# Layer 0's V pass over 208 dense tokens with a second drawn group, and the early group's dots and half of its rows in the U passes

## The chip, the cores and the metric

One NeuronCore of a Trainium2 chip runs the whole program. The metric is the device time of one execution in microseconds (us). Three runs of the kernel before were timed, and one more execution was taken with the hardware profiler; every row quoted below is from that one. Engines are named as in the profile: PE is the matrix engine (PEld its weight load), DVE the vector engine, ACT the scalar engine, POOL the GpSimd engine, SP the engine that issues most of the DMA transfers.

## The reference

A two-layer encoder for 256 tokens, to which 16 learned meta tokens are prepended (272 tokens, width 1024). Layer 0 mixes tokens with a gated recurrence, layer 1 with a Conformer convolution module; each is followed by PEER, a retrieval among 16,384 experts per layer, and every sublayer ends in a LayerNorm. PEER is where nearly all the time goes:

```python
s1, i1 = lax.top_k(scores[:, :, 0], PEER_TOPK)
s2, i2 = lax.top_k(scores[:, :, 1], PEER_TOPK)
cand = (s1[..., :, None] + s2[..., None, :]).reshape(c, PEER_HEADS, PEER_TOPK * PEER_TOPK)
s, flat = lax.top_k(cand, PEER_TOPK)
expert = idx1 * PEER_N_KEYS + idx2
g = jax.nn.softmax(s.astype(jnp.float32), axis=-1).astype(xc.dtype)
act = jax.nn.gelu(jnp.einsum('chkd,cd->chk', expert_u[expert], xc))
return jnp.einsum('chk,chkd->cd', g * act, expert_v[expert])
```

So each token picks 16 experts in each of 8 heads, takes a dot product with each picked row of U, and adds up the picked rows of V with these weights. All tables are float32.

## The kernel before

**Dense passes.** For most tokens PEER is computed densely: the product with all 16,384 rows of U, a mask of gate weights g, and the product with all rows of V. U and V of a layer are each streamed from HBM as 128 tiles (index j) of 128x1024 float32, 512 KB. A tile comes into `raw` (four buffers, issued by SP in program order), ACT rounds it to `hi` (L145), DVE or POOL forms the rest `lo` = raw - hi (L152), and PE multiplies with both parts. One j of the U pass is 24 matmuls of `nu` columns (L180). One j of the V pass is 8 matmuls `hi` x [w_hi, w_lo] of 2n columns (L749) and 8 matmuls `lo` x w_hi of n columns (L753). `nu` and n are the tokens taken densely: `DENSE_U` = 240 in both layers, `DENSE_V` = 224 in layer 0 and 192 in layer 1.

**The stages.** In each layer U is passed in two halves, called U1 (j below `JA` = 64, function `u_store`) and U2 (j from 64, `u_out`), then comes V. During U2 the gates g are built in chunks of 8 tokens (`g_unit`, `one_hot`): per chunk DVE compares, multiplies and weighs (L672, L679, L680, L659), and PE does 16 matmuls (L689, L690). `chunks` covers n tokens: 28 chunks in layer 0, 24 in layer 1.

**Tokens outside the dense passes** go in groups of `FEW` = 16 tokens; 16 tokens by 8 heads fill the 128 partitions, so one rank k of the 16 is one gather of 128 rows of 4 KB (512 KB), issued by POOL (`few_rows`, L1039). There are three kinds. An *early* and a *late* group gather their U rows and take the dots on DVE (`few_mult`, L1046); a *drawn* group lies inside the 240 dense U tokens, so its activations are dumped to a table in HBM (`few_dump`, L730 and L731) and drawn from it, rank by rank (`few_draw`, L1055 and L1056). All of them gather 16 V rows and add them up on DVE (`few_add`: L1078 the first, L1080 the others); 16 matmuls per group (L788) put the sum into the accumulators of the V pass.

- Layer 0 before: early 256, late 240, drawn 224.
- Layer 1 before: early 240, no late one, drawn 224, 208 and 192.

**Where the group work stands.** The early group takes 10 dots in U1, from j = 48, and 6 in U2. All other gathers are put into V by `few_plan`: a list of rows, spread evenly over the j from 4 to 111 with two slots of run-up. The list has 64 rows in both layers. Row buffers (`rows`) are three deep in V and U1 and single in U2. DVE runs its instructions in order, so a dot or add whose row has not landed holds back the `lo` behind it. `LO_FROM` = 41 is the j of U1 from which DVE makes `lo` in place of POOL.

**Scores of the groups.** A group with tokens below 256 gets its expert numbers (`pos`) and softmax weights (`z`) through HBM: `few_spread` writes them, `few_fetch` reads them back with one row per partition. For `z` both are issued by POOL, at the end of U1.

**SBUF for the groups.** `few_load` brings the group's inputs `wide` for the dots. The early group's are loaded twice, once for U1 and again at the beginning of U2 into a pool that opens there.

The tables that steer this, and the slots of V:

```python
DENSE_U, DENSE_V = (240, 240), (224, 192)
EARLY, LATE, DRAWN = ((256,), (240,)), ((240,), ()), ((224,), (224, 208, 192))
DOTS_FROM, DOTS, AHEAD, LO_FROM = 48, 10, 2, 41
slots = len(rows) + ahead
at = [begin + s * (NK - 4 * JG - begin) // slots for s in range(slots)]
```

## Time and profile before

| | us |
|---|---|
| three timed runs | 1786.73, 1794.49, 1797.14 |
| median | 1794.49 |
| the profiled execution, device time | 1794.43 |
| its span, first to last instruction | 1792.6 |
| layer 0: U1, U2, V begin at about | 174, 350, 552 |
| layer 1: U1, U2, V begin at about | 1078, 1255, 1459 |
| mean granted PE clock | 0.994 |

| engine | busy us | share |
|---|---|---|
| PE | 1737.4 | 97% |
| DVE | 1479.4 | 83% |
| ACT | 902.9 | 50% |
| POOL | 595.6 | 33% |

The device time stands 1.8 us above the span. Matmuls are pipelined, so a busy PE need not be a PE at its best pace: the pace is read from the distance between starts. The window rows give the busy time of each engine with the number of its instructions in brackets, then the granted clock, the mean busy share of the 16 DMA engines and the bytes they moved.

### The profile page before, as it was taken

What the parts mean: (1) busy time and instruction counts of PE and PEld (TensorE: products, weight loads), DVE (VectorE), ACT (ScalarE), POOL (GpSimd) and SP (SyncE); (2) the same over time, 40 slices, a digit from 0 to 9 for tenths busy, and PEclk for the clock granted to TensorE, in tenths of its full rate; (3) what the DMA queues carried; (4) which work ended last, traced back from release to release, by engine and by line L of the source; (5) the groups of instructions that cost most, each with busy time, mean ns of one, the idle gap of its engine ahead of it and who ended that gap; (6) DMA issues with size and microseconds to landing.
All of it is one profiled execution on the core that took longest, in us unless ns stands there. A gap on an engine that the chain in (4) does not pass through costs nothing.

```text
span 1792.6 us, 35062 instructions
## 1 busy us (share of the span) xinstructions
PE 1737.4 (97%) x13452; PEld 1675.9 (93%) x13452; DVE 1479.4 (83%) x2780; ACT 902.9 (50%) x1491; POOL 595.6 (33%) x408
## 2 busy tenths in 40 slices
PE   8999999999999999999998999999899999999996
PEld 6899999999999999999887899999899999999996
DVE  7786985899997888787799869947899878888876
ACT  5554454454444545885531645444445454544452
POOL 1101993310002445431000018952211026667420
PEclk9999999999999999999999999999999999999998
DMA  5446667865557999998541356567666569999984
GB/s 200 165 140 170 187 202 235 289 218 190 171 174 266 332 327 327 322 327 283 188 141 59 106 186 180 190 236 262 223 211 196 176 219 339 343 341 347 338 314 149
DMA packets 121112, 415.41 MB, mean 232 GB/s; under 512 B 17712, under 2 KB 19056, under 8 KB 120816
## 3 DMA queue, kind: packets, MB, share of 16 engines
q1 hardware_dynamic: 94128, 324.94, 54.4%
q0 software_dynamic: 26816, 88.23, 13.2%
q8 instruction: 106, 1.74, 0.4%
q14 instruction: 62, 0.51, 0.1%
HBM read 403.98 MB, written 9.13 MB: 230 GB/s over the span
## 4 chain that ended last, share of the span: by engine, by line
PE 77%; DVE 11%; DMA 5%; ACT 3%; issue 2%; POOL 1%; DVEq 0%; POOLq 0%; SPq 0%; ACTq 0%
PE u L180 42%; PE acc L749 16%; PE acc L753 10%; DMA raw<-peer_v 4%; PE u L216 3%; DVE lo L152 2%; DVE cy L1250 2%; DVE odd L1250 2%; PE g L689 1%; PE g L690 1%; ACT hi L145 1%; POOL lo L152 1%; PE sps L578 1%; PE acc L788 1%; DVE x L363 1%
## 5 line engine op out<-in xcount | busy, mean ns | idle before, releaser
L145 ACT ACTIVATE hi<-raw 128x1024 fp32r<-128x1024 f32 x556 | 588.3, 1059 | 617.2 <-PE u L180 212.8
L152 DVE TENSOR_TENSOR lo<-raw,hi 128x1024 fp32r<-128x1024 f32 x474 | 577.1, 1222 | 161.5 <-PE u L180 88.9
L180 PE MATMUL u<-xs,hi 128*128 128x240 f32 (+2 forms) x4544 | 570.5, 277 | 0.6 <-DVE xs L379 0.6
L180 PEld LDWEIGHTS u<-xs,hi 128*128 128x128 f32 x4544 | 539.3, 190 | 1.5 <-DVE xs L379 1.0
L749 PE MATMUL acc<-w,hi 128*128 128x448 f32 (+1 forms) x1984 | 422.8, 355 | 2.4 <-DVE w L264 1.8
L749 PEld LDWEIGHTS acc<-w,hi 128*128 128x128 f32 x1984 | 347.7, 189 | 14.3 <-DVE w L264 2.2
L180 PE MATMUL u<-xs,lo 128*128 128x240 f32 (+2 forms) x2272 | 309.5, 277 | 9.9 <-DVE lo L152 6.9
L180 PEld LDWEIGHTS u<-xs,lo 128*128 128x128 f32 x2272 | 282.0, 190 | 11.8 <-DVE lo L152 7.4
L753 PEld LDWEIGHTS acc<-w,lo 128*128 128x128 f32 x2048 | 265.7, 191 | 18.3 <-DVE lo L152 13.9
L753 PE MATMUL acc<-w,lo 128*128 128x224 f32 (+1 forms) x2048 | 270.4, 273 | 9.6 <-DVE lo L152 8.4
L152 POOL TENSOR_TENSOR lo<-raw,hi 128x1024 fp32r<-128x1024 f32 x82 | 210.4, 2580 | 105.4 <-ACT hi L145 76.0
L1039 POOL DMA_INDIRECT rows<-peer_v,ids x112 | 178.5, 1594 | 189.7 <-DVE few_out L1080 115.8
L1039 POOL DMA_INDIRECT rows<-u_rows,ids x48 | 67.3, 1402 | 218.6 <-DVE rows L1046 165.6
L1080 DVE SCALAR_TENSOR_TENSOR few_out<-rows,act,few_out 128x1024 f32<-128x1024 f32 x105 | 134.6, 1281 | 3.7 <-DMA rows<-peer_v,ids 3.7
L216 PE MATMUL u<-x,raw 128*128 128x272 f32 x480 | 115.1, 399 | 5.8 <-DMA x<-h 5.8
L216 PEld LDWEIGHTS u<-x,raw 128*128 128x128 f32 x480 | 92.8, 194 | 25.9 <-DMA raw<-w_in 5.2
L730 POOL COPY own<-act_b 128x512 f32<-128x512 f32 (+2 forms) x12 | 10.3, 863 | 247.7 <-ACT act_b L705 230.9
L1056 POOL DMA_INDIRECT act<-own,turn x64 | 74.0, 1157 | 26.0 <-issue 16.5
L696 ACT ACTIVATE act_b<-g 128x488 f32<-128x488 f32 (+35 forms) x52 | 20.2, 389 | 104.1 <-DVE act_b L659 90.6
L371 POOL TENSOR_SCALAR xs<-x,par 128x272 fp32r<-128x272 f32 (+1 forms) x4 | 3.5, 882 | 185.1 <-DVE x L363 185.1
L672 DVE TENSOR_TENSOR AB<-iota,iT 128x2048 f16<-128x2048 f16 x52 | 63.5, 1225 | 0.1
L1046 DVE SCALAR_TENSOR_TENSOR rows<-rows,wide 128x1024 f32<-128x1024 f32 x48 | 58.4, 1217 | 5.2 <-DMA rows<-u_rows,ids 5.2
(283 smaller groups left out, 1794.5 us busy)
## 6 DMA issues: line engine op xcount, KB each, us to landing
raw<-peer_u SPq DMA_DIRECT2D x256, 512.0 KB
raw<-peer_v SPq DMA_DIRECT2D x248, 512.0 KB
raw<-w_query SPq DMA_DIRECT2D x28, 512.0 KB
raw<-pw SPq DMA_DIRECT2D x22, 512.0 KB
raw<-w_in SPq DMA_DIRECT2D x16, 512.0 KB
raw<-w_out SPq DMA_DIRECT2D x8, 512.0 KB
raw<-peer_v SPq DMA_DIRECT2D x16, 256.0 KB
own<-own POOLq DMA_DIRECT2D x12, 256.0 KB
```

What stands on the lines that cost most here:

```text
L145: self.act_hi = nc.scalar.activation(hi, raw, AF.Copy).ins
L152: i = e.tensor_tensor(lo[:, s], raw[:, s], hi[:, s].bitcast(F32), op=OP.subtract)
L180: self.mm = nc.tensor.matmul(ps[:, :n], l[:, k, :], xs(k, r)[:, :n], start=start, stop=stop)
L216: self.mm = self.nc.tensor.matmul(ps[:, :n], raw[:, k, :], x[:, k, :n], start=k == 0, stop=k == NB - 1)
L672: nc.vector.tensor_tensor(AB.rearrange("p x c (a b) -> p (x c) a b", b=2), keys, iT[:, c0 // HC].rearrange("p x c b -> p (x c) b")[:, :, N ...
L749: self.mm = nc.tensor.matmul(acc[b][:, :2 * n].rearrange("p (a t) -> p a t", a=2), hi, w[:, :, :n], start=j == 0, stop=j == NK - JG - 1, s ...
L753: self.mm = nc.tensor.matmul(main[b][:, :n], hi if p_ else lo, w[:, i, :n], start=False, stop=j == NK - 1 and not p_, skip_group_check=True)
L1039: self.nc.gpsimd.indirect_dma_start(out=t, out_offset=None, in_=table, in_offset=bass.IndirectOffsetOnAxis(ap=few["ids"][:, i, k:k + 1], a ...
L1046: self.nc.vector.scalar_tensor_tensor(t, t, 1.0, few["x"], op0=OP.mult, op1=OP.mult, accum_out=few["act"][:, k:k + 1])
L1056: self.nc.gpsimd.indirect_dma_start(out=few["act"][:, k:k + 1], out_offset=None, in_=few["table"].rearrange("p j (t o) -> (p j t) o", o=1) ...
L1080: nc.vector.scalar_tensor_tensor(few["out"], t, w, few["out"], op0=OP.mult, op1=OP.add)
L1250: nc.vector.scalar_tensor_tensor(z, h, w, z, op0=OP.mult, op1=OP.add)
```

## The change

Layer 0's dense V shrinks from 224 to 208 tokens, and the 16 tokens from 208 become a second drawn group there. In both layers the early group takes its dots from j = 41, 14 of them in U1 and 2 in U2, and 8 of its 16 V rows are gathered and added in U2 (`ROWS`), so that its weights (`few_weigh`) are needed there. The rows in V become 72 in layer 0 (64 + 16 - 8) and 56 in layer 1 (64 - 8). DVE takes over `lo` from j = 34. The `z` scores go over SP in place of POOL, the spread after the last load of U1 and the fetch after the load of j = 70. `wide` of the early group is loaded once, into a pool (`kp`) that lives through the layer, and that buffer becomes the place of its sum; the other groups' sums alternate between `kp` and the pool of V (`home`), which now holds one `wide` and not two. All row gathers are held in one order on POOL (`last_rows`).

```diff
-DENSE_U, DENSE_V = (240, 240), (224, 192)
-EARLY, LATE, DRAWN = ((256,), (240,)), ((240,), ()), ((224,), (224, 208, 192))
-DOTS_FROM, DOTS, AHEAD, LO_FROM = 48, 10, 2, 41
+DENSE_U, DENSE_V = (240, 240), (208, 192)
+EARLY, LATE, DRAWN = ((256,), (240,)), ((240,), ()), ((224, 208), (224, 208, 192))
+DOTS_FROM, DOTS, ROWS, AHEAD, LO_FROM = 41, 14, 8, 2, 34
...
                     if j == LO_FROM:
-                        for few in early:
-                            self.few_load(sp, few, "kept", 1)
+                        with tc.issue_after(self.last_load):
+                            self.few_load(kp, early[0], "kept")
...
-                    if j == JA - 6 - len(picked):
-                        with tc.issue_after(last.ins):
-                            self.few_spread(nc.gpsimd, near, "z", picked[0][3][:, None])
+                    if j == JA - 1:
+                        with tc.issue_after(self.last_load):
+                            self.few_spread(nc.sync, near, "z", picked[0][3][:, None])
...
-                    if j == JA - 2:
-                        with tc.issue_after(last.ins):
-                            self.few_fetch(nc.gpsimd, near, "z")
...
-                self.few_load(rp, early[0], "kept", 1)
...
+                    done = 2 + 4 * (TOPK - DOTS)
+                    if i == 6:
+                        with tc.issue_after(self.last_load):
+                            self.few_fetch(nc.sync, near, "z")
+                    if i == done:
+                        nc.scalar.activation(early[0]["act"], early[0]["act"], AF.Gelu_apprx_tanh)
+                    if i == done + 2:
+                        with tc.issue_after(self.dve_lo.ins):
+                            self.few_weigh(early[0], scale)
+                    k, step = divmod(i - done - 4, 4)
+                    if step == 0 and 0 <= k < ROWS:
+                        early[0]["rows"][k] = self.few_rows(rp, early[0], 1, k, 1)
+                    if step == 2 and 0 <= k < ROWS:
+                        with tc.issue_after(self.dve_lo.ins):
+                            self.few_add(early[0], k, kp, "kept")
...
-    def few_plan(self, vp, early, late, drawn, scale, layer, ahead=2):
+    def few_plan(self, kp, vp, early, late, drawn, scale, ahead=2):
         rows = [(few, i, k) for few in early + late + drawn for i in range(2)
-                for k in range(0 if i or few in late else TOPK, TOPK)]
+                for k in range((ROWS if few in early else 0) if i else 0 if few in late else TOPK, TOPK)]
+        for i, few in enumerate(late + drawn):
+            few["home"] = (vp, "wide") if (i + len(late)) % 2 == 0 else (kp, "kept")
+        for few in early:
+            few["home"] = kp, "kept"
```

**Layer 1, POOL, from the end of its `lo` in U1.** The rows are POOL's instructions in order; `rows<-u_rows` are the early group's dots, `z` the scores, `own` the dumps of a drawn group. Before:

```order
L152 TENSOR_TENSOR lo<-raw,hi 128x1024 x41
L1039 DMA rows<-u_rows,ids_12497 128x1024 x8
L1018 DMA z_240_12502<-z 16x8x16
L1018 DMA z_224_12509<-z 16x8x16
L1018 DMA z_208_12516<-z 16x8x16
L1018 DMA z_192_12523<-z 16x8x16
L1022 DMA z_12499<-z_240_12502 128x16
L1022 DMA z_12505<-z_224_12509 128x16
L1022 DMA z_12512<-z_208_12516 128x16
L1022 DMA z_12519<-z_192_12523 128x16
L1039 DMA rows<-u_rows,ids_12497 128x1024 x3
```

After:

```order
L152 TENSOR_TENSOR lo<-raw,hi 128x1024 x34
L738 COPY own<-act_a 128x512
L739 DMA own_224_15166<-own 128x512
L1049 DMA rows<-u_rows,ids_12566 128x1024 x15
L738 COPY own<-act_a 128x512
```

The eight `z` transfers that stood between the gathers of the dots are gone from POOL, and one dump stands ahead of all of them.

**Layer 0, DVE, the end of U1 and the first gate chunks of U2.** `rows,act<-rows,wide` is a dot, `AB`, `Bl` the one-hot work of two chunks, `glT` the last piece of the scores. Before:

```order
L965 TENSOR_TENSOR z<-z,sm 128x16
L1035 COPY z_1621<-z 128x16
L152 TENSOR_TENSOR lo<-raw,hi 128x1024 x2
L1046 SCALAR_TENSOR_TENSOR rows,act_1620<-rows,wide 128x1024
L152 TENSOR_TENSOR lo<-raw,hi 128x1024
L1046 SCALAR_TENSOR_TENSOR rows,act_1620<-rows,wide 128x1024
L672 TENSOR_TENSOR AB<-iota,iT 128x2048 x2
L679 TENSOR_TENSOR Bl<-AB,glT 128x1024
L680 TENSOR_TENSOR AB<-AB,ghT 128x1024
L152 TENSOR_TENSOR lo<-raw,hi 128x1024 x5
```

After:

```order
L973 TENSOR_TENSOR z<-z,sm 128x16
L1043 COPY z_1621<-z 128x16
L152 TENSOR_TENSOR lo<-raw,hi 128x1024
L1056 SCALAR_TENSOR_TENSOR rows,act_1620<-rows,wide 128x1024
L668 TENSOR_TENSOR AB<-iota,iT 128x2048 x2
L675 TENSOR_TENSOR Bl<-AB,glT 128x1024
L676 TENSOR_TENSOR AB<-AB,ghT 128x1024
L152 TENSOR_TENSOR lo<-raw,hi 128x1024 x7
```

One dot fewer stands ahead of the one-hot work, and the block `AB`, `AB`, `Bl`, `AB` between two `lo` is unchanged.

More of the change, by code (lines that the diff above doesn't have):

```diff
@@ L711, in u_out @@
                     if step == 0 and DOTS <= k < TOPK:
-                        with tc.issue_after(self.lo_ins.ins):
-                            early[0]["rows"][k] = self.few_rows(rp, early[0], a["u_rows"], 0, k, 1)
+                        early[0]["rows"][k] = self.few_rows(rp, early[0], 0, k, 1)
                     if step == 2 and DOTS <= k < TOPK:
@@ L741, in peer @@
                 vp = row_pool.__enter__()
-                self.few_plan(vp, early, late, drawn, scale, layer)
+                self.few_plan(kp, vp, early, late, drawn, scale)
                 acc = [self.bank(NB - 1 - b, f"acc{b}") for b in range(NB)]
@@ L1035, in few_soft, with few_rows @@
         self.nc.vector.tensor_copy(few["z"], self.softmax(sp, few["fv"], P, 1))
-    def few_rows(self, pool, few, table, i, k, bufs):
+    def few_rows(self, pool, few, i, k, bufs):
         t = pool.tile([P, D], F32, tag="rows", name="rows", bufs=bufs)
-        self.nc.gpsimd.indirect_dma_start(
-            out=t, out_offset=None, in_=table,
-            in_offset=bass.IndirectOffsetOnAxis(ap=few["ids"][:, i, k:k + 1], axis=0))
+        table = self.a["peer_v"].rearrange("l a b d -> (l a b) d") if i else self.a["u_rows"]
+        with self.tc.issue_after(self.last_rows or self.lo_ins.ins), self.tc.issue_after(self.lo_ins.ins):
+            self.last_rows = self.nc.gpsimd.indirect_dma_start(
+                out=t, out_offset=None, in_=table,
+                in_offset=bass.IndirectOffsetOnAxis(ap=few["ids"][:, i, k:k + 1], axis=0)).ins
         return t
@@ L1051, in few_dot @@
         if k < hi:
-            few["rows"][k] = self.few_rows(pool, few, self.a["u_rows"], 0, k, ahead + 1)
+            few["rows"][k] = self.few_rows(pool, few, 0, k, ahead + 1)
     def few_draw(self, few, k):
@@ L1063, in few_gelu, with few_load @@
             self.warm(AF.Abs_reciprocal_sqrt)
-    def few_load(self, pool, few, tag="wide", bufs=2):
-        few["x"] = pool.tile([P, D], F32, tag=tag, name="wide", bufs=bufs)
+    def few_load(self, pool, few, tag):
+        few["x"] = pool.tile([P, D], F32, tag=tag, name="wide", bufs=1)
         self.nc.sync.dma_start(few["x"], few["kept"].rearrange("h t d -> (h t) d"))
@@ L1076, in few_add @@
         if k == 0:
-            few["out"] = vp.tile([P, D], F32, tag="wide", name="few_out", bufs=2)
+            few["out"] = pool.tile([P, D], F32, tag=tag, name="few_out", bufs=1)
             nc.vector.tensor_scalar(few["out"], t, w, None, op0=OP.mult)
@@ L1080, in few_add @@
             nc.vector.scalar_tensor_tensor(few["out"], t, w, few["out"], op0=OP.mult, op1=OP.add)
-    def few_plan(self, vp, early, late, drawn, scale, layer, ahead=2):
-        tables = self.a["u_rows"], self.a["peer_v"].rearrange("l a b d -> (l a b) d")
+    def few_plan(self, kp, vp, early, late, drawn, scale, ahead=2):
         rows = [(few, i, k) for few in early + late + drawn for i in range(2)
-                for k in range(0 if i or few in late else TOPK, TOPK)]
+                for k in range((ROWS if few in early else 0) if i else 0 if few in late else TOPK, TOPK)]
[3 more added lines that the diff above has]
+            few["home"] = kp, "kept"
         begin = 4
@@ L1107, in step @@
                 if i == 0 and "loaded" not in few:
-                    few["loaded"] = self.few_load(vp, few)
-                few["rows"][k] = self.few_rows(vp, few, tables[i], i, k, ahead + 1)
+                    few["loaded"] = self.few_load(vp, few, "wide")
+                few["rows"][k] = self.few_rows(vp, few, i, k, ahead + 1)
         self.steps = [(t, lambda s=s: step(s)) for s, t in enumerate(at)]
```

8 lines of the change are left out of this document (3 added, 5 removed).

## The prediction

> **What bounds the kernel now.** I read the page's shares and slices first, then the chain of work that ended last, then windows of the stages, then single rows where a stage starves.
>
> ```profile
> span 1792.6 us, 35062 instructions
> PE   8999999999999999999998999999899999999996
> DMA  5446667865557999998541356567666569999984
> PE 77%; DVE 11%; DMA 5%; ACT 3%; issue 2%; POOL 1%; DVEq 0%; POOLq 0%; SPq 0%; ACTq 0%
> ```
>
> PE is nearly always busy and holds 77% of the chain, so the time is PE's pace plus PE's gaps. The transfers are full in two places, slices 13 to 18 and 34 to 39, the V passes. These two windows of the accumulator's instructions lie inside them:
>
> ```profile
> 565.20:840.60 275.40, 273.13 (x1746) 259.65 (x1746) 0.00 (x0) 1.00 0.91 325
> 1477.70:1735.20 257.50, 250.80 (x1715) 246.19 (x1714) 0.00 (x0) 1.00 0.94 341
> ```
>
> The columns are length, PE, PEld and DVE (busy time and instructions), clock, DMA share, GB/s. A j has 16 matmuls and each group's sum 16 more, so the first holds 107 j (1746 = 1712 + 2 sums + 2) at 275.4 / 107 = 2.574 us, the second 104 j (1664 + 3 sums + 3) at 2.476 us. How fast PE could go there, the starts of its batches show:
>
> ```profile
> 692.92 1.78 PE L749 MATMUL acc<-w,hi 128*128 128x448 f32 x8
> 694.54 1.05 PE L753 MATMUL acc<-w,lo 128*128 128x224 f32 x8
> 695.42 0.37 PE L749 MATMUL acc<-w,hi 128*128 128x448 f32 x1
> 1601.03 1.60 PE L749 MATMUL acc<-w,hi 128*128 128x384 f32 x8
> 1602.46 1.04 PE L753 MATMUL acc<-w,lo 128*128 128x192 f32 x8
> 1603.34 0.91 PE L749 MATMUL acc<-w,hi 128*128 128x384 f32 x4
> 643.75 1.70 PE acc L788 x16
> 645.44 1.70 PE acc L749 x8
> ```
>
> Start to start, eight `hi` take 1.62 us at 448 columns and 1.43 us at 384; eight `lo` take 0.88 us at 224 and at 192 alike. PE's own pace is 2.50 us per j in layer 0's V and 2.31 in layer 1's; a sum costs 1.69 us (last two rows). With sums, 2.50 + 2 x 1.69 / 107 = 2.53 of the 2.574 in layer 0 is PE's: it is PE-bound, with 0.04 of stalls. In layer 1 it is 2.31 + 3 x 1.69 / 104 = 2.36 of 2.476: there 0.12 us per j is lost, at 341 GB/s. Layer 1's V is bound by transfers.
>
> **The change, part by part**, against the profiled execution's own 1794.4 us (span 1792.6 plus 1.8), which is also the median of the runs.
>
> *Layer 0's V on PE.* 32 columns fewer in each `hi` matmul save half of 1.62 - 1.43, 0.095 us per j; the `lo` matmuls, by the two equal rows, save nothing (bounds for them: 0 to 0.06 us per j, 0.88 x 16 / 224). PE's pace becomes 2.405, or 124 x 0.095 = 11.8 us less over the 124 j that have this form, and a fourth sum gives 1.7 back: -10.1 us if PE alone decided. The Trainium skill, page "TensorE: Matmul & The Clock Gate", section "Back-to-back issue gap", puts the gap at N / 2.4 + 2.5 ns, by which the `lo` matmuls would save another 8 x 16 / 2.4 = 53 ns per j, 6.6 us in the pass. The two `lo` rows contradict it: 110 ns each at both widths.
>
> *Layer 0's V on the transfers.* A V tile and a gathered row are 512 KB each (0.524 MB). Slots stand over 108 j: 66 before, one per 1.636 j, so 1.611 tiles per j or 0.845 MB; 74 after, one per 1.459 j, 1.685 tiles, 0.883 MB. At PE's new pace with sums (2.405 + 0.06) that asks for 358 GB/s. The most a long stretch delivered is the 341 of layer 1, where 0.845 / 2.36 = 358 was asked as well. At 341 a j takes 0.883 / 0.341 = 2.59 us, against 2.574 now: over the 105 j with rows +1.7 us, and the 19 j without rows go 0.095 faster, -1.8. I take **0 us** for this pass: what PE gains the gathers take. Bounds: -10 (PE decides) and +8 (331 GB/s, ten below layer 1's mean: 2.67 us per j).
>
> *Layer 1's V.* 58 slots over 108 j, one per 1.862: 1.537 tiles, 0.806 MB, which at 341 GB/s is 2.363 us per j. PE needs 2.36, so both limits meet; layer 0's V has stood just so (0.845 / 2.53 = 334 asked) and lost 0.04 us per j. I take 2.40 against 2.476: 104 x 0.076 = **-7.9 us**; bounds -12 (no stall) and -3 (three quarters of the stalls stay).
>
> *The end of U1 in layer 1.* POOL's queue is what the order rows above change.
>
> ```profile
> 1242.74 2.21 POOL L1022 DMA_DIRECT2D z<-z  x4 [3.41 <-DMA z<-z]
> 1245.26 1.86 POOL L1039 DMA_INDIRECT rows<-u_rows,ids  x1 [0.30 <-DVE glT L1137]
> 1251.19 1.23 DVE L1046 SCALAR_TENSOR_TENSOR rows<-rows,wide 128x1024 f32<-128x1024 f32 x1 [3.82 <-DMA rows<-u_rows,ids]
> 1254.92 1.22 DVE L1046 SCALAR_TENSOR_TENSOR rows<-rows,wide 128x1024 f32<-128x1024 f32 x1 [1.36 <-DMA rows<-u_rows,ids]
> 1256.19 2.36 DVE L672 TENSOR_TENSOR AB<-iota,iT 128x2048 f16<-128x2048 f16 x2
> 1261.47 0.78 PE L180 MATMUL u<-xs,lo 128*128 128x240 f32 x2 [4.90 <-DVE lo L152]
> 1238.00:1258.00 20.00, 18.12 (x159) 17.62 (x157) 14.65 (x23) 8.73 (x15) 7.38 (x10) 1.00 0.68 236
> 1258.00:1278.00 20.00, 16.52 (x136) 16.46 (x137) 13.93 (x18) 7.51 (x13) 7.71 (x10) 0.83 0.63 221
> 330.00:350.00 20.00, 19.35 (x170) 19.07 (x171) 19.66 (x41) 10.97 (x23) 5.72 (x7) 1.00 0.81 280
> 350.00:370.00 20.00, 18.49 (x180) 18.24 (x179) 16.87 (x23) 9.37 (x17) 4.43 (x6) 1.00 0.81 274
> ```
>
> POOL stands 3.41 us for a `z` spread to land, the gathers go out late, DVE stands 3.82 and 1.36 us for their rows with `lo` queued behind, and PE stands 4.90 us. The two windows lose 1.88 + 3.48 us of PE time and, the granted clock being 0.83 in the second, 0.17 x 20 = 3.4 more: 8.8 us. The same place in layer 0 (330 to 370), with two groups' `z` in place of four's, loses 0.65 + 1.51 = 2.2 us and no clock. With `z` off POOL I expect layer 1 to look like layer 0, whose loss comes of the one-hot block between two `lo`, which stays: **-6.6 us**; bounds -8.8 and 0. On SP the `z` transfers now stand among the loads: the spread is behind the load of j = 63, seven loads ahead of the fetch, and its softmax is finished some five j earlier, so SP should not stand; behind it are the raw loads, 2.7 us apart, and four buffers cover one late landing.
>
> *U2 of layer 0.* Two chunks fewer.
>
> ```profile
> 367.57 5.43 PE u L180 x48
> 373.91 5.44 PE u L180 x48
> 400.00:450.00 50.00, 50.00 (x500) 49.77 (x499) 48.22 (x76) 25.30 (x57) 2.83 (x2) 1.00 0.58 195
> 270.00:290.00 20.00, 20.00 (x181) 20.00 (x180) 5.14 (x14) 10.23 (x16) 12.45 (x6) 1.00 0.66 204
> L1080 DVE SCALAR_TENSOR_TENSOR few_out<-rows,act,few_out 128x1024 f32<-128x1024 f32 x105 | 134.6, 1281 | 3.7 <-DMA rows<-peer_v,ids 3.7
> L152 DVE TENSOR_TENSOR lo<-raw,hi 128x1024 fp32r<-128x1024 f32 x474 | 577.1, 1222 | 161.5 <-PE u L180 88.9
> ```
>
> Between the two chain rows a chunk's 16 matmuls take 6.34 - 5.43 = 0.91 us: **-1.8 us**.
>
> *Costed at nothing.* The adds in U2 replace four dots by eight adds, net 4 x 1.28 = 5.1 us of DVE per layer. From 400 to 450 DVE was busy 48.22 of 50 us with dots among the `lo`, and PE 50.00 of 50: that is the cover, and it is thin (uncovered, +5 per layer). In U1 four more dots and seven more `lo`, some 13 us, fall where DVE was busy 5.14 of 20 us (270 to 290). Draws, dumps and the gathers go to POOL, 33% busy, and the gathers now in U1 and U2 meet DMA shares of 0.58 to 0.66 there. The new waits (fetch of `z` ahead of `few_weigh`) have about 18 us, six j, to land.
>
> *Sum:* 0 - 7.9 - 6.6 - 1.8 = -16.3, so **1778 us**.
>
> **The rivals.**
>
> *V of layer 0 stays PE-bound.* Then the pass gives its 10 us and the time is 1768. For it: from 0.91 to 0.94 the DMA engines still had idle time. Against: layer 1 asked the same 358 GB/s and got 341. The Trainium skill, page "DMA: Bandwidth & Descriptors", section "Measured (HBM→SBUF, 128 partitions, SWDGE, issued from GpSimd)", gives 425 GB/s for 16 MB from a single core, which would make this the case; no stretch quoted here shows such a rate. Chance 0.2.
>
> *The stall at the end of layer 1's U1 stays,* because the one-hot block, not the late rows, makes it: 1778 + 6.6 = 1785. The 3.82 us of waiting ahead of the block speak against it. Chance 0.12.
>
> *Rows come late in layer 0's V, and it ends slower.* A row can go out when the add three slots earlier frees its buffer: 3 x 1.636 x 2.574 = 12.6 us before its use now, 3 x 1.459 x 2.59 = 11.3 then, less POOL's issue. DVE takes rows in order, so each late one holds `lo` and then PE. In the trace DVE waited 3.7 us in all at 105 adds. The gain is gone when each of the 72 rows is 0.23 us late on average, and the time is 0.5% worse from 0.35 us; at 0.4 us it is 1778 + 29 = 1807. Chance 0.1.
>
> *The U passes pay for the moved work* (DVE at its limit in U2 of both layers, 2 x 5.1 us uncovered): 1788. Against: PE had no gap at DVE's 96%. Chance 0.08.
>
> **How the numbers follow.** The forecast (1771 to 1785) has 0.5, the rivals 0.2, 0.12, 0.1 and 0.08. 0.5% is about what a measurement of this kernel can tell from no change. Within it (1785.5 to 1803.5) lie the fourth rival, half of the second and a piece of the forecast's upper edge; slower is the third: 0.7 faster, 0.21 the same, 0.09 slower. The range takes in the second case of layer 0's V and the stall that stays together with the fourth rival's cost, and leaves the late rows out: 1764 to 1792.
>
> **What would show it.** In the profile after: `hi` batches in layer 0's V near 1.53 us start to start and `lo` still 0.88; that pass near 2.58 us per j at about 341 GB/s with ACT waiting for `raw`; layer 1's V at 2.40 us or less; no wait of DVE for `rows<-u_rows` at the end of layer 1's U1 and a granted clock of 1.00 there; PE without gaps in U2. Wrong it would be if DVE waits for `rows<-peer_v` grow to tens of us, or if layer 0's V runs above 2.65 us per j.

## The result, and the profile after

The changed kernel takes 1809.80 us (median of four runs, 1808.52 to 1814.66); the kernel before, with one more run, 1795.82. The ratio is 1.0096 with a 95% interval of 1.0069 to 1.0124: by the medians 14 us slower, by the ratio 17, where 16 us less were forecast. The profiled execution took 1808.52 us. From its page:

```profile
span 1805.7 us, 35138 instructions
PE   8999999899999999999998999999998998999996
DMA  5545668766657999998541356688665568999984
PE 68%; DVE 12%; DMA 10%; issue 4%; ACT 3%; POOL 2%; SPq 0%; POOLq 0%; DVEq 0%; another core or an unknown queue 0%; ACTq 0%
```

PE's share of the chain fell from 77% to 68%, and DMA's rose from 5% to 10%. PE's slice 29, the end of layer 1's U1, is full again, but three others are newly under 9: the eighth (316 to 361 us, the end of layer 0's U1), the 31st (1354 to 1399 us, layer 1's U2) and the 34th (1490 to 1535 us, early in layer 1's V). By passes, from the starts of the matmuls in both traces (U is U1 and U2 together, up to V's first matmul; V runs to its last `hi`):

| | before | after | forecast | measured |
|---|---|---|---|---|
| layer 0, U | 378.8 | 382.5 | -1.8 | +3.7 |
| layer 0, V | 318.9 | 323.6 | 0 | +4.7 |
| layer 1, U | 380.8 | 385.5 | -6.6 | +4.7 |
| layer 1, V | 304.7 | 304.6 | -7.9 | -0.1 |
| all else in the span | 409.4 | 409.5 | 0 | +0.1 |

**Layer 0, end of U1.** Rows of the timeline: start, length, engine, line, instruction, and in brackets the idle time before it with what ended it.

```profile
335.65 1.50 SPq L1026 DMA_DIRECT2D z<-z  x3
335.12 1.22 DVE L1056 SCALAR_TENSOR_TENSOR rows<-rows,wide 128x1024 f32<-128x1024 f32 x1
340.39 0.17 DVE L962 TENSOR_TENSOR z<-fv 128x16 f32<-128x16 f32 x1 [4.04 <-DMA z<-z]
340.52 1.23 DVE L152 TENSOR_TENSOR lo<-raw,hi 128x1024 fp32r<-128x1024 f32 x1
341.81 1.17 PE L180 MATMUL u<-xs,lo 128*128 128x240 f32 x8 [2.88 <-DVE lo L152]
345.76 1.16 PE L180 MATMUL u<-xs,lo 128*128 128x240 f32 x8 [0.99 <-DVE lo L152]
352.18 1.17 PE L180 MATMUL u<-xs,lo 128*128 128x240 f32 x8 [3.47 <-DVE lo L152]
```

DVE stands 4.04 us at a tiny instruction, the first of the early group's softmax. It writes the tile `z`, which has two buffers and is needed here for the third time, and the first buffer is only free when the spread, issued on SP at 335.65, has read it. The next `lo` stands behind it, and PE behind that. The last gap, 3.47 us against 1.51 before, is at the one-hot block: as the order rows above show, one `lo` stands ahead of the block where three did.

**Layer 1, U2.** The timeline of POOL, then of DVE and PE:

```profile
1364.56 1.55 POOL L738 COPY own<-act_b 128x512 f32<-128x512 f32 x1
1372.35 0.62 POOL L738 COPY own<-act_b 128x512 f32<-128x512 f32 x1 [5.35 <-DMA own<-own]
1377.70 2.03 POOL L738 COPY own<-act_b 128x512 f32<-128x512 f32 x1 [3.87 <-DMA own<-own]
1386.44 0.62 POOL L738 COPY own<-act_a 128x512 f32<-128x512 f32 x1 [5.86 <-DMA own<-own]
1390.26 0.62 POOL L738 COPY own<-act_a 128x512 f32<-128x512 f32 x1 [2.36 <-DMA own<-own]
1392.02 1.01 POOL L1049 DMA_INDIRECT rows<-peer_v,ids  x1 [0.30 <-issue]
1396.65 1.28 DVE L1090 SCALAR_TENSOR_TENSOR few_out<-rows,act,few_out 128x1024 f32<-128x1024 f32 x1 [10.86 <-DMA rows<-peer_v,ids]
1399.12 2.06 PE L180 MATMUL u<-xs,lo 128*128 128x240 f32 x8 [7.64 <-DVE lo L152]
```

Two windows at and behind the last of these rows (length, busy time of PE, PEld, DVE, ACT and POOL, granted clock, DMA share, GB/s):

```profile
1385.00:1395.00 10.00, 6.48 (x66) 6.26 (x64) 0.79 (x2) 1.38 (x3) 3.33 (x5) 1.00 0.46 138
1395.00:1410.00 15.00, 10.88 (x78) 10.85 (x79) 12.73 (x18) 5.92 (x14) 1.72 (x1) 0.66 0.57 191
```

Five dumps in a row stand ahead of a gather. They share one buffer, so each waits for the transfer of the one before, and the gather goes out at 1392.02. Its add waits 10.86 us, `lo` waits behind the add, PE stands 7.64 us, and then PE's granted clock is 0.66 over 15 us, another 0.34 x 15 = 5.1 us.

**Layer 1, end of U1**, where the stall was to go, in the timeline and in a window:

```profile
1255.18 2.36 DVE L668 TENSOR_TENSOR AB<-iota,iT 128x2048 f16<-128x2048 f16 x2 [0.78 <-DMA z<-z]
1260.06 1.17 PE L180 MATMUL u<-xs,lo 128*128 128x240 f32 x8 [2.57 <-DVE lo L152]
```

```profile
1258.00:1278.00 20.00, 17.94 (x167) 17.91 (x168) 13.93 (x17) 9.13 (x15) 3.85 (x6) 1.00 0.65 213
```

It did: 2.57 us in place of 4.90, and the clock stays at 1.00. But here, too, DVE waits for a spread of `z`, 0.78 us: by the kernel's pools the one-hot tile `AB` takes over memory that the softmax gives up, which no run tests.

**The V passes.** Windows of the accumulator's instructions over 112 steps, from `hi` 8 to `hi` 120, in layer 0 and layer 1 (length, PE, PEld, DVE, clock, DMA share, GB/s):

```profile
575.10:869.60 294.50, 283.20 (x1859) 277.10 (x1858) 0.00 (x0) 0.99 0.92 328
1489.70:1767.40 277.70, 271.59 (x1859) 268.75 (x1858) 0.00 (x0) 0.99 0.91 321
```

The same 112 steps of layer 1 before:

```profile
1477.80:1755.70 277.90, 271.20 (x1859) 266.60 (x1858) 0.00 (x0) 1.00 0.93 336
```

Three batches of layer 0's V in the timeline of PE:

```profile
640.62 1.69 PE L757 MATMUL acc<-w,hi 128*128 128x416 f32 x8
642.14 1.04 PE L761 MATMUL acc<-w,lo 128*128 128x208 f32 x8
643.02 1.68 PE L757 MATMUL acc<-w,hi 128*128 128x416 f32 x8
```

Groups of instructions between 560 and 870 us (busy us, mean ns, idle time before them and what ended it):

```profile
L145 ACT ACTIVATE hi<-raw 128x1024 fp32r<-128x1024 f32 x118 | 124.8, 1059 | 121.9 <-DMA raw<-peer_v 86.2 <-PE acc L757 13.5 <-DVE lo L152 9.3
L1090 DVE SCALAR_TENSOR_TENSOR few_out<-rows,act,few_out 128x1024 f32<-128x1024 f32 x53 | 68.0, 1283 | 6.4 <-DMA rows<-peer_v,ids 6.3
L761 PE MATMUL acc<-w,lo 128*128 128x208 f32 x944 | 125.0, 275 | 10.9 <-DVE lo L152 7.5 <-DVE turn L1065 2.9 <-issue 0.3
```

A step without a stall is 643.02 - 640.62 = 2.40 us, as computed. The pass runs at 294.5 / 112 = 2.63. With four sums (1.69 us each) and the pace of twenty steps without a stall, 2.402 us, the unstalled pass would be 124 x 2.402 + 4 x 1.69 = 304.6 us, so 19 us of 323.6 are stalls; before it was 124 x 2.503 + 3 x 1.69 = 315.4 of 318.9. ACT waits 86.2 us for loads of `raw`, and DVE 6.3 us for rows (`rows<-peer_v`). Layer 1's V is unchanged at 2.48 us per step on average, with the rate down from 336 to 321 GB/s for the same 112 steps. The average hides two parts. By the starts of the `hi` batches, steps 20 to 120 took 241.7 us, 4.2 less than before (245.9), and steps 12 to 20 took 25.2 us, 4.4 more than before (20.8); at the unstalled 2.333 us these eight would take 18.7. One step alone, from 1509.1 to 1515.4 us, took 6.2: this is the new dent in slice 34.

### The profile page after: what moved, and what is told of

Read it like the earlier page. It is cut to its first block, busy times and chain, and to the rows that moved or that the text cites. A ratio compares the mean times of both kernels' runs of the same rounds, so it can differ in the third digit from the quotient of the medians.

```text
span 1805.7 us, 35138 instructions
## 1 busy us (share of the span) xinstructions
PE 1730.2 (96%) x13436; PEld 1679.5 (93%) x13436; DVE 1507.1 (83%) x2821; ACT 900.6 (50%) x1489; POOL 596.4 (33%) x424
## 4 chain that ended last, share of the span: by engine, by line
PE 68%; DVE 12%; DMA 10%; issue 4%; ACT 3%; POOL 2%; SPq 0%; POOLq 0%; DVEq 0%; another core or an unknown queue 0%; ACTq 0%
PE u L180 39%; PE acc L757 12%; PE acc L761 8%; DMA rows<-peer_v,ids 4%; DMA raw<-peer_v 4%; DVE lo L152 3%; PE u L216 3%; DVE cy L1263 2%; DVE odd L1263 2%; PE g L685 1%; DMA own<-own 1%; POOL lo L152 1%; PE g L686 1%; PE sps L578 1%; ACT hi L145 1%
## 5 line engine op out<-in xcount | busy, mean ns | idle before, releaser
L152 DVE TENSOR_TENSOR lo<-raw,hi 128x1024 fp32r<-128x1024 f32 x488 | 594.1, 1222 | 130.7 <-PE u L180 53.7
L757 PE MATMUL acc<-w,hi 128*128 128x416 f32 (+1 forms) x1984 | 414.4, 351 | 3.1 <-DVE w L264 1.8
L1049 POOL DMA_INDIRECT rows<-peer_v,ids x128 | 190.7, 1490 | 359.2 <-DVE few_out L1090 193.6
L761 PE MATMUL acc<-w,lo 128*128 128x208 f32 (+1 forms) x2048 | 271.5, 274 | 18.0 <-DVE lo L152 13.3
L152 POOL TENSOR_TENSOR lo<-raw,hi 128x1024 fp32r<-128x1024 f32 x68 | 176.8, 2619 | 101.2 <-ACT hi L145 74.4
L1090 DVE SCALAR_TENSOR_TENSOR few_out<-rows,act,few_out 128x1024 f32<-128x1024 f32 x120 | 153.7, 1281 | 20.9 <-DMA rows<-peer_v,ids 20.8
L1049 POOL DMA_INDIRECT rows<-u_rows,ids x48 | 63.0, 1312 | 144.2 <-DVE rows L1056 97.8
L1066 POOL DMA_INDIRECT act<-own,turn x80 | 99.8, 1248 | 28.3 <-issue 21.9
L692 ACT ACTIVATE act_b<-g 128x488 f32<-128x488 f32 (+39 forms) x50 | 19.4, 388 | 117.0 <-DVE act_b L655 98.1
L738 POOL COPY own<-act_b 128x512 f32<-128x512 f32 (+2 forms) x15 | 16.1, 1082 | 151.0 <-ACT act_b L701 124.3
```

The source lines that it names most:

```text
L152: i = e.tensor_tensor(lo[:, s], raw[:, s], hi[:, s].bitcast(F32), op=OP.subtract)
L757: self.mm = nc.tensor.matmul(acc[b][:, :2 * n].rearrange("p (a t) -> p a t", a=2), hi, w[:, :, :n], start=j == 0, stop=j == NK - JG - 1, s ...
L761: self.mm = nc.tensor.matmul(main[b][:, :n], hi if p_ else lo, w[:, i, :n], start=False, stop=j == NK - 1 and not p_, skip_group_check=True)
L1049: self.last_rows = self.nc.gpsimd.indirect_dma_start(out=t, out_offset=None, in_=table, in_offset=bass.IndirectOffsetOnAxis(ap=few["ids"][ ...
L1066: self.nc.gpsimd.indirect_dma_start(out=few["act"][:, k:k + 1], out_offset=None, in_=few["table"].rearrange("p j (t o) -> (p j t) o", o=1) ...
L1090: nc.vector.scalar_tensor_tensor(few["out"], t, w, few["out"], op0=OP.mult, op1=OP.add)
```

## The experiments

The theory after this reading: two new waits, each at the head of an in-order queue (the `z` buffer, the dumps), cost some 5 and 12 us; and layer 0's V gives its gain back to late data. The rivals: DVE has too much in the U passes, wherever the waits stand; or the second drawn group is the whole cost. Ratios are to the kernel before, with 95% intervals; lengths in us are from one profiled execution each and vary by some us from one to the next, as layer 1's V shows, which is the same in the change, e1 to e4 and e6 (299.3 to 306.1).

| kernel | ratio | L0 U | L0 V | L1 U | L1 V |
|---|---|---|---|---|---|
| before | 1 | 378.8 | 318.9 | 380.8 | 304.7 |
| the change | 1.0096 (1.0069-1.0124) | 382.5 | 323.6 | 385.5 | 304.6 |
| e1 third `z` buffer | 1.0076 (1.0057-1.0095) | 378.4 | 323.3 | 383.6 | 306.1 |
| e2 dumps behind gathers | 1.0049 (1.0030-1.0068) | 384.0 | 325.7 | 377.3 | 305.2 |
| e3 early spread and e2 | 0.9992 (0.9978-1.0007) | 380.5 | 325.5 | 374.5 | 300.9 |
| e4 V of layer 0 as before | 1.0060 (1.0037-1.0082) | 388.6 | 317.0 | 384.5 | 301.9 |
| e5 before, second drawn group | 1.0030 (1.0013-1.0047) | 378.5 | 323.3 | 374.5 | 305.1 |
| e6 without its rows in V | 0.9997 (0.9980-1.0014) | 382.8 | 310.1 | 385.6 | 299.3 |
| e8 all mended, V as e4 | 0.9985 (0.9970-1.0000) | 385.7 | 315.8 | 376.4 | 300.8 |
| e9 draws paced | 1.0083 (1.0062-1.0105) | 385.6 | 323.8 | 385.4 | 306.8 |
| e10 e3, fifth `raw` in layer 1 | 1.0021 (1.0007-1.0035) | 380.6 | 322.6 | 374.0 | 310.2 |
| e11 before, `z` on SP | 0.9984 (0.9971-0.9996) | 378.9 | 317.6 | 375.5 | 309.8 |
| e12 e3, rows 3 ahead in layer 1 | 1.0000 (0.9983-1.0017) | 379.6 | 326.2 | 376.0 | 304.7 |
| e13 e3, without its draws | 1.0015 (0.9999-1.0031) | 379.4 | 325.2 | 375.9 | 304.4 |
| e16 e3, rows 3 ahead in layer 0 | 0.9994 (0.9976-1.0011) | 379.4 | 319.6 | 376.3 | 303.5 |
| e17 e3, fifth `raw` in both | 0.9915 (0.9894-0.9936) | 379.7 | 312.7 | 374.6 | 304.0 |
| e18 before, fifth `raw` in both | 0.9941 (0.9921-0.9960) | 378.7 | 314.8 | 377.9 | 297.3 |

**The two waits, each alone.**

```diff
-        z = sp.tile([P, H, K], F32, tag="z", name="z", bufs=2)
+        z = sp.tile([P, H, K], F32, tag="z", name="z", bufs=3)
```

> The changed kernel with three buffers instead of two for the softmax's result z, so that the third softmax of layer 0 (early group 256) no longer waits until the spread on SP has read the first one. Theory (late spread): DVE's wait of 4.04 us for the DMA z<-z at the end of layer 0's U1 goes, and with it most of the 3.04 + 1.15 + 3.63 us that PE stands there; the pass from 172.0 to 355.9 gets 5 us shorter (3 to 8), the whole about 1804.8. The like wait in layer 1 (0.78 us of DVE, for the one-hot tile AB) stays, since it is another tile. Rival (DVE simply has too much at that place): the wait's name changes, the pass stays within 1.5 us, the whole within 2 us of 1809.8.

Layer 0's U became 4.1 us shorter and the time 0.20% (3.6 us): near the expected size, though the intervals of the two ratios overlap. The third gap of PE stayed (3.46 us, ahead of it DVE's one-hot block with one `lo` only), so it is no part of this wait.

```diff
-                        dumps.setdefault(j1 - 1 - JA if j >= JA else 16 * g + 8 * i + 3, []).append((few, j, j1))
+                        dumps.setdefault(max(j1 - 1 - JA, 45) if j >= JA else 45 if g == 2 else 16 * g + 8 * i + 3, []).append((few, j, j1))
...
-                        few_dump(*piece)
+                        with tc.issue_after(self.last_rows): few_dump(*piece)
```

> The changed kernel with the dumps of the drawn groups in U2 placed on POOL behind the row gathers (none of the five in a row of layer 1 stands ahead of a gather). Theory (head of POOL's queue): in layer 1's U2 DVE's wait of 10.86 us for rows, PE's wait of about 7.7 us behind it and the half clock of 10.24 us that follows (about 5 us more) go; layer 1's U2 from 1263.8 to 1471.0 gets 12 us shorter (8 to 14), the whole is about 1798. Rival (U2's adds are too much for DVE or the transfers wherever the gathers stand): the same loss comes back in smaller pieces, the whole within 4 us of 1809.8.

Layer 1's U is 8.2 us shorter (its U2 10.5, of 8 to 14 expected) and the time 0.47% (8.4 us). The window from 1360 to 1460 us of this kernel:

```profile
1360.00:1460.00 100.00, 99.85 (x988) 99.36 (x987) 92.96 (x131) 47.23 (x110) 15.95 (x19) 1.00 0.64 209
```

the same window of the change:

```profile
1360.00:1460.00 100.00, 92.36 (x887) 91.78 (x886) 83.86 (x119) 42.09 (x98) 16.95 (x19) 0.95 0.59 185
```

and this kernel's group of adds between 1290 and 1465 us:

```profile
L1090 DVE SCALAR_TENSOR_TENSOR few_out<-rows,act,few_out 128x1024 f32<-128x1024 f32 x7 | 8.9, 1277 | 0.0
```

With the same adds, and no wait ahead of one, PE is busy 99.85 of 100 us at full clock, DVE 92.96: it was the queue and not DVE's work.

**Both mended, and the halves of the change.** e3 has e2's edit and, in place of another buffer, an earlier spread:

```diff
-                    if j == JA - 1:
+                    if j == JA - 8:
                         with tc.issue_after(self.last_load):
                             self.few_spread(nc.sync, near, "z", picked[0][3][:, None])
```

> The changed kernel with the dumps behind the row gathers and, besides, the spread of z on SP seven steps earlier (step 56 of U1 instead of 63), so that nothing late waits for it: neither the third softmax in layer 0 nor the one-hot tile AB in layer 1. Theory: both stalls are separate costs, so this gains what the third buffer and the moved dumps gained apart: layer 0's U1 about 187 us (191.9 in the changed kernel), layer 1's U2 about 189 (199.2), ratio to before about 1.003. Rival (SP now waits for the softmax at the head of its queue, and the loads behind it come late): U1 no shorter than 191 in either layer, or longer, ratio 1.005 or more.

The ratio fell to 0.9992, further than the 1.003 of the sum, and layer 1's U2 took 188.7 us, as expected. Layer 0's U1, up to its first one-hot matmul, fell short: it took 190.3 us, against 191.9 in the change and 187 expected. Here SP does stand at the spread, as the rival had it: 4.3 us in layer 0 (between 300 and 360 us; total, times, longest), 3.4 in layer 1.

```profile
SPq L1026 <- DVE z L973: 4.3, 1, 4.3
```

```profile
348.62 1.17 PE L180 MATMUL u<-xs,lo 128*128 128x240 f32 x8 [3.47 <-DVE lo L152]
```

DVE's wait of 4.04 us is gone, but PE's gap at the one-hot block is as it was in the change, and it is 3.5 us in e8, e16 and e17 too, where the kernel before had 1.51. In the six profiles with these two edits and 208 tokens (e3, e10, e12, e13, e16, e17) layer 0's U1 takes 189.2 to 190.4 us, before 186.6: some 3 us remain there. e1, with the spread where the change has it, took 187.7, and e5, with the second group alone, 188.3; how the 3 us divide among the earlier spread, the second group and DVE's added work is not settled.

Of the 10 us between e2 and e3, layer 0's U shows 3.5 and layer 1's 2.8; the rest lies in layer 1's V and the tail, where single executions differ as much, so it is not assigned. Apart, the two edits took back 0.67 of the 0.96%; together they bring the change level with the kernel before, to the accuracy of these runs. What the change was to win is still missing.

```diff
-DENSE_U, DENSE_V = (240, 240), (208, 192)
+DENSE_U, DENSE_V = (240, 240), (224, 192)
-EARLY, LATE, DRAWN = ((256,), (240,)), ((240,), ()), ((224, 208), (224, 208, 192))
+EARLY, LATE, DRAWN = ((256,), (240,)), ((240,), ()), ((224,), (224, 208, 192))
```

> The changed kernel with layer 0's V as before (224 dense tokens, one drawn group); moved dots and rows stay. Theory: V of layer 0 is bound by transfers once 16 more rows are drawn, so taking them out wins back the loss there and more (V 324.6 to about 312 us, 124 steps at about 2.50), while the two one-hot chunks come back in U2 (about 2 us): the whole about 1800. The stalls at the end of layer 0's U1 and in layer 1's U2 stay. Rival 1 (the second drawn group is the whole cause): at or under 1793, faster than the kernel before. Rival 2 (only the stalls cost): 1808 to 1812.

> The kernel before with only the other part of the change: layer 0's V dense for 208 tokens and the second drawn group 208 (dots and rows where they were). Theory: layer 0's V then gathers 80 groups of rows instead of 64 and is bound by transfers, about 2.68 us per step against 2.58 before, 12 us longer; U2 of layer 0 is 2 us shorter; the whole about 1806, and layer 1 as before to 2 us. Rival (the moved dots and rows are the whole loss): within 3 us of the kernel before, or faster.

e5 is the reverse of this diff on the kernel before. Neither half is the whole cost. In e4 V of layer 0 fell by 6.6 to 317.0 us, not to 312, and U of layer 0 became 6.1 us longer, not 2, so that the time fell by 0.36% (6.5 us, of 10 expected): between the theory and the second rival. In e5 V of layer 0 is 323.3, not some 331, and the time 0.30% longer, not 0.6%: eighty gathers of rows take no longer than seventy-two. The bytes per step cannot be the limit in the way the forecast had it. e8 puts the mended waits, e9's pacing and e4's V together.

> The changed kernel with all of it: dumps behind the gathers, the spread of z seven steps earlier, draws of layer 1 paced, and layer 0's V as before (224 tokens, one drawn group). Theory: the moved dots and rows are worth something once their stalls are gone: against the kernel before, layer 1's V is about 6 us shorter and the rest equal to 2 us, ratio 0.996 (0.993 to 0.999). Rival (moving DVE work into the U passes costs as much as it gives): ratio 1.000 to 1.004.

0.9985 with an interval of 0.9970 to 1.0000: in the upper part of the expected range, and no longer slower. Its parts missed: layer 1's V is 3.9 us shorter than before, not 6, and layer 0's U 6.9 longer, not equal to 2 us.

**What holds back layer 0's V.** e6, and then e13 (on e3):

```diff
-                self.few_plan(kp, vp, early, late, drawn, scale)
+                self.few_plan(kp, vp, early, late, drawn if layer else drawn[:1], scale)
```

```diff
         for few in drawn:
             lo, hi = hi, at[rows.index((few, 1, 0)) + ahead] - 3
+            if late and few["t0"] == 208:
+                few["act"] = drawn[0]["act"]
+                continue
```

> The changed kernel, 208 dense tokens in layer 0's V, but the second drawn group's draws, row gathers and adds left out (its tokens get the sums of group 224; dumps and everything else stay). Theory: the 208-token pace of 2.40 us per step is real and only the 16 more gathers with their 16 draws take it away: V of layer 0 from its first to its last big matmul 300 us (298 to 305) instead of 323.6. Rival (loads of raw, ScalarE's hi or VectorE's lo cannot keep 2.40 even with 56 gathers): V stays above 312.

> The kernel with early spread and moved dumps, with the second drawn group's 16 draws left out in layer 0 (it weighs with group 224's values); its 16 row gathers and adds stay. Theory (transfers of the 16 rows are what the 208-token pace runs into): V of layer 0 stays within 4 us of 325.5. Rival (the draws, 16 times 128 small packets and about 1 us each on POOL's queue, are the larger part of the 13.5 us that leaving the whole group out of V gave): V falls to 315 to 319.

Without the 16 rows V takes 310.1 us, between the theory's 305 and the rival's 312: the pace is real, and 13.5 of the 19 us of stalls come with the second group. Its draws cost nothing (325.2 against 325.5). There remain the 16 gathers, by their bytes, their lead or the loads beside them, and DVE's 16 adds.

```diff
-                self.few_plan(kp, vp, early, late, drawn, scale)
+                self.few_plan(kp, vp, early, late, drawn, scale, 3 - layer)
```

> The kernel with early spread and moved dumps, with the gathers of layer 0's V issued three slots ahead of their adds instead of two, with one more buffer for rows; for its memory four of the convolution's 124 diagonal tiles are made some 10 us later, in the stage behind. Theory (a gather must land within its lead: two of 74 slots over 108 steps of 2.40 us are 7.0 us, and rows land in 7.3 to 7.7 us in the median): VectorE's waits for rows in this V, 8.6 us in all, fall below 2 us, its stall at the 64th step goes, V falls from 325.5 to 314 (310 to 318). Rival (the total of bytes is the limit): V stays at 321 or more, and the waits move to the loads of raw. Everything else as in that kernel, ratio 0.993 by the theory, 0.998 to 1.002 by the rival.

```diff
-        raw = self.wp.tile([P, NB * P], F32, tag="raw", name="raw", bufs=4)
+        self.loads += 1
+        if self.extra and self.loads % 5 == 0:
+            raw = self.extra.tile([P, NB * P], F32, tag="raw5", name="raw", bufs=1)
+        else:
+            raw = self.wp.tile([P, NB * P], F32, tag="raw", name="raw", bufs=4)
...
+                    if j == 12:
+                        self.extra = extra
```

> The kernel with early spread and moved dumps, with a fifth buffer for raw in both layers' V from the 12th step on (so that no load waits at the pass's start for its memory), and the same four diagonal tiles later. Theory (layer 0's V is held up by late rows, layer 1's by late loads only a little): V of layer 0 stays at 320 to 327 us, V of layer 1 is 297 to 299 (300.9 without, 296.2 is the unstalled pace with its four sums). Rival (late loads are what holds up layer 0's V): it falls to 315 or less. Second rival (the total of bytes): both stay within 2 us of 325.5 and 300.9.

The same groups between 560 and 870 us, of e3, of e16 and of e17 (whose lines are shifted):

```profile
L145 ACT ACTIVATE hi<-raw 128x1024 fp32r<-128x1024 f32 x118 | 124.4, 1057 | 125.8 <-DMA raw<-peer_v 89.7 <-PE acc L757 20.3 <-DVE lo L152 12.0
L1090 DVE SCALAR_TENSOR_TENSOR few_out<-rows,act,few_out 128x1024 f32<-128x1024 f32 x53 | 68.0, 1282 | 7.0 <-DMA rows<-peer_v,ids 7.0
L761 PE MATMUL acc<-w,lo 128*128 128x208 f32 x936 | 124.9, 276 | 12.0 <-DVE lo L152 11.8
```

```profile
L145 ACT ACTIVATE hi<-raw 128x1024 fp32r<-128x1024 f32 x121 | 127.8, 1058 | 122.9 <-DMA raw<-peer_v 89.4 <-PE acc L757 12.1 <-DVE few_out L1090 6.7
L1090 DVE SCALAR_TENSOR_TENSOR few_out<-rows,act,few_out 128x1024 f32<-128x1024 f32 x53 | 67.8, 1279 | 0.0
L761 PE MATMUL acc<-w,lo 128*128 128x208 f32 x957 | 126.1, 274 | 11.2 <-DVE lo L152 5.9 <-DVE turn L1065 5.2
```

```profile
L150 ACT ACTIVATE hi<-raw 128x1024 fp32r<-128x1024 f32 x122 | 129.0, 1059 | 119.0 <-PE acc L764 52.5 <-DMA raw<-peer_v 40.6 <-DVE lo L157 11.2
L1102 DVE SCALAR_TENSOR_TENSOR few_out<-rows,act,few_out 128x1024 f32<-128x1024 f32 x53 | 67.9, 1282 | 8.5 <-DMA rows<-peer_v,ids 8.3
L768 PE MATMUL acc<-w,lo 128*128 128x208 f32 x978 | 128.1, 273 | 5.3 <-DVE lo L157 5.3
```

With one more slot of lead DVE no longer waits for rows at all, but PE's wait ahead of `lo` hardly falls (11.2 us against 12.0 in e3), V is only 5.9 us shorter, short of the 310 to 318 expected, and the time stays where it was. With a fifth load buffer rows are as late as ever, yet ACT's wait for `raw` falls from 89.7 us in e3 to 40.6, PE's to 5.3, V by 12.8 to 312.7, and the time by 0.77%. For layer 0's V my theory fell and its rival held: **late loads were the larger part**, with the same bytes and the same adds (e16 has e17's four later diagonal tiles too, so these do not make the difference), and they were late because only four may be under way or in use at a time. For layer 1's V the theory missed: 304.0 us, where 297 to 299 was expected. A stretch of e17's layer 0's V (length, PE, PEld, DVE, ACT, POOL, clock, DMA share, GB/s) shows what the transfers can do:

```profile
600.00:820.00 220.00, 215.94 (x1439) 214.29 (x1438) 195.56 (x219) 144.97 (x233) 139.59 (x88) 0.99 0.96 353
```

At 0.9915 this is the lowest ratio of the study.

**Layer 1's V.** e9 puts empty places behind the early group's rows; e12 (`2 + layer` in place of e16's `3 - layer`) gives this pass's rows one more slot, e10 its loads e17's buffer from the first step on, both on e3.

```diff
+        rows[ROWS:ROWS] = [] if late else [None] * 8
```

> The changed kernel with eight empty places put behind the early group's eight rows in layer 1's V, so that the first drawn group's 16 draws are issued over 24 steps as in the kernel before, not over 13. Theory: the early stalls of this V (DVE's wait of 3.60 us for rows, PE's gaps of 1.5, 1.5 and 3.2 us and the half clock behind them, at 1490 to 1518) come from draws that are bunched on POOL's queue among the gathers; V of layer 1 then takes 298 us (295 to 301) instead of 304.6, the whole 6 us less. Rival (the transfers limit this V in total, wherever the draws stand): V stays at 303 to 306 and the loss turns up later in smaller pieces.

> The kernel with early spread and moved dumps, with the gathers of layer 1's V issued three slots ahead of their adds instead of two (one more buffer for rows, in that layer alone). Theory (rows that land late stop VectorE): DVE's waits for rows go, V of layer 1 falls by 3 us (2 to 6) to about 298. Rival (raw's loads are what comes late, and one more gather in flight only delays them): V stays at 300 or gets longer by up to 4 us.

> The kernel with early spread and moved dumps, with a fifth buffer for the loads of raw in layer 1's V alone (every fifth load goes to it). Theory (loads come late because each waits for a buffer that VectorE's lo frees, and every gather beside it lengthens its landing): with one more load ahead V of layer 1 falls from 300.9 to about 293 us (290 to 296; 289.3 would be 124 steps at the unstalled 2.333). Rival (the transfers' total is the limit): V stays at 299 to 303.

In us, by the starts of the `hi` batches, this V shows what became of each:

| layer 1's V, steps | 12 to 20 | 20 to 120 | whole |
|---|---|---|---|
| before | 20.8 | 245.9 | 304.7 |
| the change | 25.2 | 241.7 | 304.6 |
| e3 | 18.8 | 244.2 | 300.9 |
| e9 | 18.7 | 248.9 | 306.8 |
| e10 | 18.7 | 244.2 | 310.2 |
| e12 | 19.0 | 246.4 | 304.7 |
| e17 | 25.3 | 241.6 | 304.0 |
| e18 | 18.7 | 240.1 | 297.3 |

With the draws paced the early stall is gone, and its time comes back later, where e9's other 48 rows stand as close as before: the rival held. But e3, with the change's own code for this V, shows no early stall either, so bunched draws alone do not make it, and its cause stays open. The lead of the rows gave nothing (e12, ratio 1.0000). e10 fell outside both its theory and its rival: it got longer, mostly in one place. A row of its timeline, one of its waits of SP's queue between 1440 and 1485 us (total, times, longest), and one of its groups between 1482 and 1775 us:

```profile
1466.20 2.95 ACT L150 ACTIVATE hi<-raw 128x1024 fp32r<-128x1024 f32 x3 [8.14 <-DMA raw<-peer_v]
```

```profile
SPq L140 <- DMA own<-own: 7.0, 1, 7.0
```

```profile
L150 ACT ACTIVATE hi<-raw 128x1024 fp32r<-128x1024 f32 x120 | 127.3, 1061 | 141.5 <-PE acc L763 114.7 <-DMA raw<-peer_v 14.0 <-remote 3.3
```

At the beginning of V SP waited 7.0 us for a dump's transfer, `own`, whose memory the fifth buffer had taken over, and ACT stood 8.14 us. After that ACT waits 14.0 us for loads, where e3 has 112.2 in the same group and stretch; yet steps 20 to 120 take 244.2 us in both, so with 56 rows PE got no faster by it. Because of the 8.14 us e17 starts its fifth buffer at the 12th step.

**The same edits on the kernel before.** e11 has `few_spread` for `z` at `JA - 8` and `few_fetch` at i = 6, both with `nc.sync`; e18 has e17's buffer.

> The kernel before with one edit: the spread of z goes out on SP at step 56 of U1 and its fetch on SP in U2, instead of both on POOL among the dots' gathers; everything else as before. Theory of the prediction: POOL's z work holds back the last gathers at the end of layer 1's U1 in every run, so this wins 6.6 us (ratio about 0.9963). Rival (the stall of 5.07 us with the half clock behind it, 8.8 us, is there only in some executions: with the same POOL order the run with the second drawn group showed 2.57 us and no half clock): ratio 0.9985 to 1.001.

> The kernel before with nothing but the fifth buffer for raw in both layers' V from the 12th step on (and four of the convolution's diagonal tiles made in the stage behind). Theory (the change pays once the loads are early: its V of layer 0 has a lower unstalled pace, 2.402 against 2.503 us per step): V of layer 0 falls only from 318.9 to 316 (315.6 is the unstalled pace with three sums), V of layer 1 from 304.7 to 298 to 302, the ratio is 0.995 to 0.998, above the 0.9915 of the mended change with the same buffer. Rival (the buffer alone does it): ratio 0.990 to 0.993.

`z` off POOL is worth 0.16% (2.9 us; 0.04 to 0.29%), under half of the 6.6 us. The fifth buffer alone is worth 0.59%, between theory and rival, against 0.85% with the mended change; the intervals (0.9921 to 0.9960 and 0.9894 to 0.9936) overlap, so the mended change is worth about a quarter of a per cent on top, and that is not settled. A stretch of layer 1's V (columns as in e17's), in the kernel before and then in e18:

```profile
1480.00:1680.00 200.00, 194.03 (x1328) 190.28 (x1327) 173.74 (x200) 98.43 (x100) 129.89 (x96) 1.00 0.95 341
1480.00:1680.00 200.00, 200.00 (x1388) 200.00 (x1387) 181.31 (x205) 104.11 (x105) 136.81 (x97) 1.00 0.97 357
```

With all its 64 rows layer 1's V takes 297.3 us, 1.2 above its unstalled 124 x 2.333 + 4 x 1.69 = 296.1. It moves 357 GB/s over 200 us in which PE never stands, where the kernel before moves 341.

## Why the prediction was wrong

Four steps failed. The dumps' wait on POOL and the spread's on `z` were put at nothing; a stalled rate was taken for a ceiling in layer 0's V; and layer 1's V got a stall at its start that was not in the sum.

- **Layer 0's V on PE: right.** 2.40 us per step for 2.405, `hi` batches at 1.52 us start to start for 1.53, `lo` still 0.88, and the fourth sum. The rule that the prediction weighed (the Trainium skill, page "TensorE: Matmul & The Clock Gate", section "Back-to-back issue gap") is given there for an isolated matmul, and in a stream of weight loads and matmuls, as here, that section lets both set the spacing. At 208 columns, too, the trace shows no gain of `lo`.
- **Layer 0's V on the transfers: the size inside its bounds (+4.7 of -10 to +8), the reason wrong.** The step that failed is "At 341 a j takes 2.59 us": it took the rate of a stalled stretch for a ceiling. e17 moves the same tiles and rows in 312.7 us, at 353 GB/s over 220 us, and e18 moves 357 over 200 us of layer 1's V without a stall of PE, as against 341 in the same stretch with four buffers. So 341 was what the stalls left, not a limit. What makes e17's last 8 us above 304.6 stays open; bytes may be part of it, the DMA share being 0.96.
- **Layer 1's V: -7.9 became -0.1.** The pace came: steps 20 to 120 took 2.417 us each with all sums, for 2.40. But before they had taken 2.459, not 2.476, so that this was worth 4.2 us, and the stall in steps 12 to 20, for which the sum had no term, cost 4.4. The reason was wrong besides: "Layer 1's V is bound by transfers" is contradicted by e18, which reaches 297.3 with all rows in place. The eight profiles of this V with 56 rows and equal code (the change, e1 to e4, e6, e13, e16) average 303.2 us, the three with 64 rows and four buffers (before, e5, e11) 306.5, so the rows are worth some 3 us.
- **End of layer 1's U1: right in the profile, over-sized in the runs.** The late rows are gone from DVE, the clock is 1.00, and U1 up to the first one-hot matmul is 6.0 us shorter (186.4 for 192.4). But the 8.8 us were read from one execution as if every one had them; e5, with `z` on POOL as before, shows the same place like this:

```profile
1260.51 1.17 PE L180 MATMUL u<-xs,lo 128*128 128x240 f32 x8 [2.41 <-DVE lo L152]
```

- **"SP should not stand": true of the change, and beside the point.** The spread's new time was asked of SP, its queue, and not of those who wait for its source tile. Two did, and in layer 0 that cost about 4 us (4.1 in e1's profile, 3.6 in its runs). Sent earlier, in e3, the spread did make SP stand.
- **"Draws, dumps and the gathers go to POOL, 33% busy": the costliest step.** A busy share says nothing of an in-order queue whose head waits for a transfer. In the changed kernel's order five dumps on POOL stood ahead of a gather; no wait was priced there. From its first one-hot matmul to V layer 1's U2 takes 199.2 us after and 188.4 before; in the runs e2 gave 8.4 us back.
- **The adds in U2, net 5.1 us of DVE per layer: rightly costed at nothing**, as e2's window of layer 1 shows (PE 99.85 of 100). **The dots and `lo` added to U1, also put at nothing:** in layer 0 U1 stays some 3 us longer than before even in the mended kernels, with PE's gap at the one-hot block at 3.5 us for 1.51; the prediction had that gap as unchanged. **U2 of layer 0: right**; from its first one-hot matmul to V it took 190.6 us after and 192.3 before, -1.7 for -1.8.
- **The rivals.** That layer 0's V stays PE-bound did not come about (19 us of stalls). The one of late rows there saw a real mechanism, but not the larger one: DVE waited 6.3 us for rows there, and e16, which took such waits away, gained 5.9 us of V and nothing in the time. The slower end came in the main from the U passes, +8.4 of the +13.1, and no rival had these slower than before. The range's upper end was said to take in the staying stall together with the fourth rival's cost; that would be 1778 + 6.6 + 10.2 = 1795, above 1792.

In sum, the forecast's -16.3 against +13.1 of the span: +4.7 from layer 0's V, +7.8 from layer 1's V, +5.5 from layer 0's U, +11.3 from layer 1's U (its U2 alone is 10.8 longer), +0.1 elsewhere.
